# Tree attention on one core: four V copies two steps later, and 768 KB of the last stores moved from SyncE's queue to GpSimd's

## The chip, the cores and the metric

The kernel runs on one core of one Trainium2 chip. A core has TensorE (PE in the profile; its weight loads are PEld), VectorE (DVE), ScalarE (ACT), GpSimd (POOL) and SyncE (SP), which run their own queues of instructions and meet through semaphores, and 16 DMA engines that move data between device memory and the core's memories. GpSimd, SyncE and ScalarE issue the transfers; those of GpSimd go through one software queue, those of SyncE and ScalarE through a hardware queue each. The metric is the device time of one execution in microseconds. Before the change it is 134.9 us, the median of 3 runs (134.57 to 135.15).

## What is computed

Attention over 8 x 12 = 96 heads of 512 positions and 64 dimensions, where position i may attend only to itself and to its ancestors in a binary tree (the parent of i is (i - 1) // 2):

```python
scores = np.einsum('bhqd,bhkd->bhqk', Q, K) * scale
scores = scores + (1 - mask) * (-1e9)          # mask[i, j] = 1 for j = i and i's ancestors
weights = np.exp(scores - np.max(scores, axis=-1, keepdims=True))
weights = weights / (np.sum(weights, axis=-1, keepdims=True) + 1e-10)
return np.einsum('bhqk,bhkd->bhqd', weights, V).astype(np.float32)
```

Q, K, V and the output are float32, 12.6 MB each.

## The kernel before, in words

**Pairs and steps.** The 96 heads are taken as 48 pairs. From pair 8 on the heads of two neighbouring pairs are interleaved, so that pairs 2n and 2n + 1 fill the four heads 4n to 4n + 3, and pair 2n has the first and third of them. One step of the main loop (variable `i`, 0 to 48) does, on PE, the scores of pair i (`scores1`, `scores2`: codes for the mask, L458 and L491, and keys times queries, L466 and L501), then the value products of pair i - 1 (`values`, L551), then the turn (transposition) of K or Q for two pairs: in an odd step i the K of pairs i + 3 and i + 4 (`wide_k`, L401), in an even step the Q of pairs i + 2 and i + 3 (`wide_q`, L433). ScalarE takes the exponentials (L476, L507). VectorE normalizes pair i - 1 (`norm`: reciprocal L581, product L582), copies the turned K or Q out of PSUM (L412, L416, L420 for K, L441 for Q), and does its share of the V copies. There is one PSUM buffer for the value products, so the products of pair i wait for the normalization of pair i - 1.

**V copies.** The schedule is written out by hand; each engine takes its instructions in the order in which the program issues them. V is loaded in blocks of 16 heads (8 pairs), in three pieces by partition ("upper", "even", "odd"), and then rearranged by `spread` (L336) into value tiles that PE reads; block o serves pairs 8o to 8o + 7. There are two sets of value tiles, used in turn. `BY_VECTOR` and `BY_SCALAR` say which copies are issued in which step for blocks 0 to 3; from block 4 on `STEADY_VECTOR` and `STEADY_SCALAR` do, by the step's number modulo 8, for the block after the one whose step it is. "M" (reads all three pieces) and "Y" (reads "even" and "odd") are VectorE's, "Z0" and half of "Z1" (both read "upper") ScalarE's. GpSimd makes the "top" copies, "X", which overwrites part of what M wrote and so comes after both halves of M, and half of "Z1".

**GpSimd's queue.** `pool_program` is the list of all loads, GpSimd's V copies and most stores, in one fixed order; `ready` says from which step on the head of that list may be issued. Loads cast float32 to bfloat16 on the way. K and Q are loaded 8 heads at a time (`load_k`, `load_q`, L251), V by `load_rows` (L280). Eight semaphores serve this queue in turn, so that each transfer is issued only when the one issued eight before it has landed.

**Stores.** `norm` writes a quad of four heads (two pairs), 512 KB, kept in one of 22 buffers. `store` (L590) writes a quad, or some of its heads, to device memory. GpSimd stores quads 0 to 21 but for quad 19, at first between loads and 56 heads behind, the rest one after another at the end of its list. Quad 19 (pairs 38 and 39) is stored by SP at step 41 in two transfers by rows, 60 and 68 of the 128 (`store_apart`, L600 to L606). The pairs 44, 45 and 46 are each stored by SP as soon as they are normalized (256 KB each, steps 45 to 47), and the two heads of pair 47 by SP and by ScalarE.

Of the kernel before, what the change touches and what calls it, by code (L numbers as in the profile page):

```python
# [119 lines left out]
def kernel(  # L120
# [7 lines left out]
    nc = tc.nc  # L128
    B, H, S, D = Q.shape
    P = nc.NUM_PARTITIONS  # L130
    assert S == 512 and D == 64 and P == 128 and (B * H) % 4 == 0
    scale = float(1.0 / np.sqrt(D))
    NH = B * H
    NQ = NH // 4
    NP = 2 * NQ
    WIDE = 8
    KB, VB = 8, 16
# [14 lines left out]
    Or = out.rearrange("b h (p t) d -> p (b h) (t d)", t=4)  # L152
# [58 lines left out]
    NV = 2  # L211
# [17 lines left out]
    qTs, kTs, kqs, obs, ets, ofs = {}, {}, {}, {}, {}, {}  # L229
# [224 lines left out]
    def scores1(i):  # L454

        sp = psS.tile([P, 2, 512], fp32, name="s1")
        for a in range(2):
            nc.tensor.matmul(  # L458
                out=sp[:, a, :],
                lhsT=(k1code if i < WIDE else k1wide)[64 * a:64 * a + CODE_ROWS, :],  # L460
                rhs=(q1code[64 * a:64 * a + CODE_ROWS, :] if i < WIDE
                     else q1wide[64 * a:64 * a + CODE_ROWS, :, :]),
                start=True, stop=False,
            )
        for a in range(2):
            nc.tensor.matmul(  # L466
                out=sp[:, a, :], lhsT=keys(i, a, TOP),
                rhs=qTs[i][64 * a:64 * a + 64, :, :].rearrange("p t c -> p (t c)"),
                start=False, stop=True,
            )  # L470
        et = etpool.tile([P, 2, 4, 128], bf16, name="e1")
        nc.scalar.activation(  # L472
            out=et[:, :, :, :].rearrange("p a t c -> p (a t c)"),
            in_=sp[:, :, :].rearrange("p a c -> p (a c)"),
            func=AF.Exp, scale=scale,
        ) if i < WIDE else nc.scalar.activation(  # L476
            out=et[:, :, :, :].rearrange("p a t (r u) -> p a (t r) u", u=2),
            in_=sp[:, :, :].rearrange("p a (u c) -> p a c u", u=2),
            func=AF.Exp, scale=scale,
        )  # L480
        ets[i] = et
# [31 lines left out]
    def scores2(i):  # L513
        if i >= WIDE:
            return scores2_wide(i)
        sp = psS.tile([P, 2, 4, 128], fp32, name="s2")
        flat = sp[:, :, :, :].rearrange("p a t c -> p a (t c)")
        for a in range(2):
            nc.tensor.matmul(
                out=sp[:, a, :, 32:128], lhsT=k2code[64 * a:64 * a + CODE_ROWS, :],  # L520
                rhs=q2code[64 * a:64 * a + CODE_ROWS, :].rearrange(
                    "p (t c) -> p t c", t=4
                )[:, :, 32:128],
                start=True, stop=False,
            )
        for t, lo, hi in ((2, 32, 192), (0, 192, 256), (3, 288, 448), (1, 448, 512)):
            for a in range(2):
                nc.tensor.matmul(
                    out=flat[:, a, lo:hi], lhsT=keys(i, a, TILE2[t]),
                    rhs=qTs[i][64 * a:64 * a + 64, :, :].rearrange("p t c -> p (t c)")[:, lo:hi],  # L530
                    start=False, stop=t == 1, skip_group_check=t in (2, 3),
                )
        nc.scalar.activation(
            out=e2s[i % NE][:, :, :, 32:128].rearrange("p a t c -> p (a t) c"),
            in_=sp[:, :, :, 32:128].rearrange("p a t c -> p (a t) c"),
            func=AF.Exp, scale=scale,
        )
# [59 lines left out]

    APART, APART_AT, APART_ROWS = 19, 41, 60

    def store_apart():  # L600

        for p0, p1 in ((0, APART_ROWS), (APART_ROWS, P)):
            nc.sync.dma_start(
                out=Or[p0:p1, 4 * APART:4 * APART + 4, :],
                in_=ofs[APART][p0:p1, :, :, :].rearrange("p h t d -> p h (t d)"),
            )  # L606

    def pool_program():

        ops = [  # L610
            (load_k, 2, 2), (load_q, 2, 2), (load_v, 0, 4), (load_v, 4, 4),
            (load_k, 4, 2), (load_k, 6, 2), (load_q, 4, 2), (load_k, 8, 4),
            (load_q, 6, 2), (load_q, 8, 4), (load_v, 8, 8), (load_k, 12, 4),
            (load_q, 12, 4), (load_k, 16, 4), (load_rows, 1, "upper"),
            (load_q, 16, 4), (load_rows, 1, "even"), (load_k, 20, 4), (load_rows, 1, "odd"),
            (load_q, 20, 4), (load_k, 24, 8), (load_q, 24, 4), (load_rows, 2, "upper"),
            (load_q, 28, 4), (load_k, 32, 4), (load_rows, 2, "even", "odd"),
            (load_q, 32, 8), (load_k, 36, 4), (load_rows, 3, "upper"),
            (load_k, 40, 8), (load_q, 40, 8),
            (load_rows, 3, "even", "odd"), (spread_top, 2, 0, 16), (spread_top, 3, 0, 4), (load_q, 48, 4),  # L620
            (spread_top, 3, 4, 8), (load_k, 48, 8), (load_q, 52, 4), (spread_top, 3, 8, 12),
            (load_rows, 4, "upper"), (spread_top, 3, 12, 16),
        ]
        loaded, stored = 72, 0
        for h in range(56, NH, KB):
            top = [(spread_top, h // VB + 0)] if h % VB == 8 and 4 <= h // VB + 0 < NH // VB else []
            ops += [(load_k, h, KB)] + top + [(load_q, h, KB)]
            while loaded < min(h + 32, NH):
                names = ("even", "odd") if loaded % VB else ("upper",)
                ops.append((load_rows, loaded // VB) + names)  # L630
                loaded += KB
            if top:
                o = h // VB
                ops.append((spread_pool, (o, "X", 0, 16), (o, "Z1", 8, 16)))
            while 4 * stored + 4 + BEHIND <= h + KB:
                ops.append((store, nc.gpsimd, stored))
                stored += 1
        ops += [(store, nc.gpsimd, q) for q in range(stored, NQ - 2) if q != APART]
        return ops

    def ready(op, i):

        f, args = op[0], op[1:]
        if f in (load_k, load_q):
            return 2 * (i + 3) >= args[0] + args[1] - 4 * KB
        if f is load_v:
            return True
        if f is load_rows:
            return 2 * i >= VB * (args[0] - 2)
        if f is spread_pool:  # L650
            return 2 * i >= VB * (args[0][0] + 1 - NV) + 6
        if f is spread_top:
            return 2 * i >= VB * (args[0] + 1 - NV)
        return 2 * i >= 4 * (args[1] + 1)
# [21 lines left out]
        22: [(3, "Y", 0, 8)],  # L676
        23: [(3, "X", 8, 16)],
        24: [(3, "Y", 8, 16)],
    }
    BY_SCALAR = {  # L680
# [18 lines left out]
    }  # L699

    STEADY_VECTOR = {0: [("M", 0, 8)], 2: [("M", 8, 16)], 4: [("Y", 0, 8)], 6: [("Y", 8, 16)]}
# [2 lines left out]
    def spread_by(copy, table, steady, i):  # L704

        o, j = divmod(i, 8)
        todo = table.get(i, [])
        if 4 <= o + 1 < NH // VB:
            todo = todo + [(o + 1,) + piece for piece in steady.get(j, [])]
        for args in todo:  # L710
            spread(copy, *args)
# [25 lines left out]
    for i in range(NP + 1):  # L737
        steps = FIRST[i] if i < len(FIRST) else "SVK" if i % 2 else "SVQ"
        for step in steps:
            if step == "S" and i < NP:  # L740
                scores1(i)
                scores2(i)
            if step == "V" and i >= 1:
                values(i - 1)
                norm(i - 1)
                valued = True
            if step == "K" and kdone < NP:
                kdone = turn("kst", kdone)
            if step == "Q" and qdone < NP:
                qdone = turn("qst", qdone)  # L750
            if step == "W":
                nc.scalar.copy(
                    out=codes[64:64 + CODE_ROWS, 1280:1536], in_=codes[0:CODE_ROWS, 1280:1536]
                )
            if step == "X":
                spin("s1" if valued else "ob", 2)
            if step == "D":
                spread_by(nc.vector.tensor_copy, BY_VECTOR, STEADY_VECTOR, i)
            if step == "A":
                spread_by(nc.scalar.copy, BY_SCALAR, STEADY_SCALAR, i)  # L760
        if "D" not in steps:
            spread_by(nc.vector.tensor_copy, BY_VECTOR, STEADY_VECTOR, i)
        if "A" not in steps:
            spread_by(nc.scalar.copy, BY_SCALAR, STEADY_SCALAR, i)
        pool(i)
        if i == APART_AT:
            store_apart()
        if i >= NP - 3 and i < NP:
            store(nc.sync, (i - 1) // 2, (i - 1) % 2, 2, 2)
    assert not program  # L770
    store(nc.sync, NQ - 1, 1, 1)
# [31 lines left out]
```

## Time and profile before

| what | value |
|---|---|
| median of 3 runs | 134.9 us (134.57 to 135.15) |
| the profiled execution's own time | 134.59 us |
| its span, first to last instruction | 132.7 us |
| busy: PE / VectorE / ScalarE / GpSimd | 115.9 / 101.8 / 102.3 / 70.8 us |
| device memory read and written | 37.94 and 12.58 MB, 381 GB/s over the span |
| granted clock of TensorE, mean | 0.962 |
| last matmul ends | 127.15 us from the span's start |
| last store is issued (ScalarE) | 128.42 us |

The profile is of one execution. Its times count from the first instruction. A row of a timeline has the start, the time taken, the engine, the line of the kernel, the operation, what it writes and reads, how many were merged, and in brackets how long the engine stood idle ahead of it and what ended that. "PEclk" is the clock granted to TensorE, in tenths of full speed in the slices and as a fraction in the windows. "DMA share" is the busy time of the 16 DMA engines over the stretch; it can be above 1 where packets overlap. GB/s counts the bytes as written, so that a load from float32 to bfloat16 counts half of what is read.

### The profile page before, as it was taken

The page shows a single profiled execution, that of the slowest core. Times are in us where ns is not written, and L with a number is a line of the kernel's source. Part 1 is how long each engine was busy: PE and PEld are TensorE (multiplying, and loading weights), DVE is VectorE, ACT ScalarE, POOL GpSimd, SP SyncE. Part 2 cuts the span into 40 slices and gives each one's busy share as a digit, 9 for nine tenths or more (in the row PEclk, how much of TensorE's full clock was granted, in tenths as well). Part 3 has the DMA queues.
Part 4 walks back from the last instruction along what each step waited for, and adds up shares of the span by engine and source line. Part 5 has one row for each costly group of instructions (what it writes and reads, how often), then busy time and mean ns, then how long its engine had stood idle before and what let it go on. Part 6 is the DMA issues. An engine that isn't in the chain of part 4 may idle for free.

```text
span 132.7 us, 5554 instructions
## 1 busy us (share of the span) xinstructions
PE 115.9 (87%) x2414; PEld 80.5 (61%) x2417; DVE 101.8 (77%) x253; ACT 102.3 (77%) x169; POOL 70.8 (53%) x110
## 2 busy tenths in 40 slices
PE   6986979999899999999989399999999997979930
PEld 2453755766675666677767267767767675656620
DVE  3439779889999999988985655888987977756360
ACT  4359577988799999979899536997997987695910
POOL 6989625355345808999413359863958524422000
PEclk9999999999999999999999756999999999999995
DMA  3999999999999999999999999999999999999992
GB/s 113 237 179 194 200 196 200 201 202 206 200 202 202 203 202 206 199 207 201 207 202 198 307 264 201 281 285 240 327 218 328 239 292 399 405 394 406 360 332 87
DMA packets 32381, 32.27 MB, mean 243 GB/s; under 512 B 1341, under 2 KB 29629, under 8 KB 32357
## 3 DMA queue, kind: packets, MB, share of 16 engines
q0 software_dynamic: 29984, 29.63, 114.4%
q1 hardware_dynamic: 1813, 1.83, 4.0%
q10 hardware_dynamic: 560, 0.46, 1.1%
q8 instruction: 19, 0.31, 0.9%
q14 instruction: 5, 0.04, 0.1%
HBM read 37.94 MB, written 12.58 MB: 381 GB/s over the span
## 4 chain that ended last, share of the span: by engine, by line
DMA 42%; PE 39%; issue 6%; ACT 4%; POOL 3%; DVE 2%; ACTq 0%; POOLq 0%
DMA vst<-in_V_dram 35%; PE ob L551 12%; DMA kst<-in_K_dram 7%; PE s L458 6%; PE ktp L401 4%; PE s L466 4%; PE qtp L433 3%; PE s L491 3%; PE s L501 3%; ACT e L507 2%; ACT e L476 2%; DVE of L582 1%; PE s L551 1%; ACT e L472 1%; DVE vt L336 1%
## 5 line engine op out<-in xcount | busy, mean ns | idle before, releaser
L476 ACT ACTIVATE e<-s 128x1024 bf16<-128x1024 f32 x40 | 40.8, 1019 | 15.1 <-PE s L466 14.8
L551 PE MATMUL ob<-vt,e 128*128 128x65 bf16 (+1 forms) x940 | 38.2, 199 | 4.8 <-DVE of L582 2.9
L551 PEld LDWEIGHTS <-e 128*128 128x128 bf16 (+1 forms) x960 | 31.0, 104 | 13.0 <-DVE of L582 3.1
L507 ACT ACTIVATE e<-s 128x384 bf16<-128x384 f32 x80 | 34.4, 486 | 0.0
L582 DVE TENSOR_TENSOR of<-ob,rec 128x512 f32<-128x512 f32 x47 | 32.5, 691 | 1.6
L590 POOL DMA_DIRECT2D out_dram<-of x21 | 16.0, 763 | 16.1 <-DVE of L582 5.0
L336 DVE COPY vt<-vst 32x1024 bf16<-32x1024 bf16 (+6 forms) x46 | 19.5, 425 | 5.5 <-issue 2.8
L458 PE MATMUL s<-codes 40*128 40x512 bf16 x96 | 19.9, 401 | 1.2 <-ACT e L472 0.4
L581 DVE RECIPROCAL rec<-ob 128x8 f32<-128x8 f32 x47 | 9.7, 206 | 13.7 <-PE ob L551 13.2
L336 POOL COPY vt<-vst 32x128 int32<-32x128 int32 (+2 forms) x32 | 15.7, 490 | 6.9 <-DMA vst<-in_V_dram 4.0
L466 PE MATMUL s<-kq 64*128 64x512 bf16 x96 | 19.0, 385 | 0.0
L280 POOL DMA_DIRECT2D vst<-in_V_dram x15 | 11.1, 742 | 10.5 <-DMA vst<-in_V_dram 6.1
L336 ACT COPY vt<-vst 32x512 int32<-32x512 int32 (+3 forms) x29 | 15.9, 550 | 1.0 <-DMA vst<-in_V_dram 0.5
L501 PEld LDWEIGHTS <-kq 64*128 64x128 bf16 x320 | 12.7, 95 | 4.5 <-issue 0.7
L501 PE MATMUL s<-kq 64*128 64x160 bf16 (+1 forms) x320 | 15.2, 210 | 0.0
L491 PE MATMUL s<-codes 40*128 40x384 bf16 x80 | 14.1, 339 | 0.9
L251 POOL DMA_DIRECT2D kst<-in_K_dram x12 | 9.0, 753 | 10.4 <-PE s L466 3.4
L401 PE MATMUL ktp<-ptile,kst 128*64 128x128 bf16 x320 | 12.9, 224 | 1.2 <-issue 0.8
L441 DVE COPY kq<-qtp 128x1024 bf16<-128x1024 bf16 x20 | 13.6, 681 | 0.0
L491 PEld LDWEIGHTS <-codes 40*128 40x128 bf16 x80 | 6.6, 96 | 11.0 <-issue 3.8
L433 PE MATMUL qtp<-ptile,qst 128*64 128x128 bf16 x320 | 13.1, 224 | 0.2 <-issue 0.2
L251 POOL DMA_DIRECT2D qst<-in_Q_dram x13 | 9.5, 731 | 5.7 <-PE s L501 3.0
(42 smaller groups left out, 123.8 us busy)
## 6 DMA issues: line engine op xcount, KB each, us to landing
out_dram<-of POOLq DMA_DIRECT2D x21, 512.0 KB, 12.6
kst<-in_K_dram POOLq DMA_DIRECT2D x8, 512.0 KB, 13.3
qst<-in_Q_dram POOLq DMA_DIRECT2D x7, 512.0 KB, 13.8
vst<-in_V_dram POOLq DMA_DIRECT2D x12, 256.0 KB, 13.0
vst<-in_V_dram POOLq DMA_DIRECT2D x6, 512.0 KB, 12.7
qst<-in_Q_dram POOLq DMA_DIRECT2D x8, 256.0 KB, 10.8
kst<-in_K_dram POOLq DMA_DIRECT2D x6, 256.0 KB, 11.6
out_dram<-of SPq DMA_DIRECT2D x3, 256.0 KB, 5.0
```

The costliest lines, as they stand in the source:

```text
L251: return nc.gpsimd.dma_start(out=kept[b][:, h0 % KB:h0 % KB + n, :, :].rearrange("p (g x) t d -> p g (x t d)", x=2), in_=wide[:, h0 // 2:( ...
L336: return copy(out=dst, in_=src)
L401: nc.tensor.transpose(out=columns(kp[64 * a:64 * a + 64, :], mixed, (256, 2), (leaves - mixed, 2), (1, 32)), in_=st[:, 2 * i % KB // 2 + a ...
L433: nc.tensor.transpose(out=halves[64 * a:64 * a + 64, :, c:c + 64], in_=st[:, 2 * i % KB // 2 + a, 4 * u + t, :], identity=ptile[:, 0:128],)
L458: nc.tensor.matmul(out=sp[:, a, :], lhsT=(k1code if i < WIDE else k1wide)[64 * a:64 * a + CODE_ROWS, :], rhs=(q1code[64 * a:64 * a + CODE_ ...
L466: nc.tensor.matmul(out=sp[:, a, :], lhsT=keys(i, a, TOP), rhs=qTs[i][64 * a:64 * a + 64, :, :].rearrange("p t c -> p (t c)"), start=False, ...
L476: ) if i < WIDE else nc.scalar.activation(
L491: nc.tensor.matmul(out=flat[:, a, :, :].rearrange("p u (t c) -> p u t c", t=4)[:, :, :, 16:64], lhsT=k2wide[64 * a:64 * a + CODE_ROWS, :], ...
L501: nc.tensor.matmul(out=flat[:, a, :, lo:hi], lhsT=keys(i, a, WTILE2[t]), rhs=qT[64 * a:64 * a + 64, :, lo:hi], start=False, stop=t == 1, s ...
L507: nc.scalar.activation(out=e2s[i % NE][:, a, :, 32:128].rearrange("p t (r u) -> p t r u", u=2), in_=flat[:, a, :, :].rearrange("p u (t r) ...
L551: nc.tensor.matmul(out=ob[lo:hi, a, 65 * t:65 * t + 65], lhsT=e[:, a, PLACE[t], lo:hi], rhs=vt[vtile[tile_v][0]][:, head(i, a) % VB, vtile ...
L582: nc.vector.tensor_tensor(out=ofs[q][:, head(i, a) % 4:head(i, a + n - 1) % 4 + 1:head(i, 1) - head(i, 0), :, :], in0=o4[:, a:a + n, :, 0: ...
```

## The change

Two things change, and nothing is computed differently.

First, VectorE's four copies of block 4 (heads 64 to 79, pairs 32 to 39). They were issued in steps 24, 26 (the halves of M), 28 and 30 (the halves of Y) by the steady table; now they are in `BY_VECTOR` at steps 26, 28, 30 and 31. ScalarE's three copies of block 4 are written out in `BY_SCALAR` at their old steps 25, 27 and 29. The steady tables begin with block 5. GpSimd's X and Z1 pieces of blocks 4 and 5 are issued one step later (`+ 8` in place of `+ 6`).

Second, the stores. Quad 22 (pairs 44 and 45) is stored by GpSimd, as the last of its list, in one transfer of 512 KB instead of two of 256 KB by SP. Of quad 19 SP stores only the first two heads, in the same 60 and 68 rows; GpSimd stores the other two heads at quad 19's place in its list, in three transfers of 9, 116 and 3 rows. SP keeps pair 46 and one head of pair 47.

```diff
+    def store_rows(eng, q, h0, *bounds):
+
+        for p0, p1 in zip(bounds, bounds[1:]):
+            eng.dma_start(
+                out=Or[p0:p1, 4 * q + h0:4 * q + h0 + 2, :],
+                in_=ofs[q][p0:p1, h0:h0 + 2, :, :].rearrange("p h t d -> p h (t d)"),
+            )
+
     def store_apart():
 
-        for p0, p1 in ((0, APART_ROWS), (APART_ROWS, P)):
-            nc.sync.dma_start(
-                out=Or[p0:p1, 4 * APART:4 * APART + 4, :],
-                in_=ofs[APART][p0:p1, :, :, :].rearrange("p h t d -> p h (t d)"),
-            )
+        store_rows(nc.sync, APART, 0, 0, APART_ROWS, P)
...
-        ops += [(store, nc.gpsimd, q) for q in range(stored, NQ - 2) if q != APART]
+        for q in range(stored, NQ - 1):
+            if q == APART:
+                ops.append((store_rows, nc.gpsimd, q, 2, 0, 9, 125, P))
+            else:
+                ops.append((store, nc.gpsimd, q))
         return ops
...
         if f is spread_pool:
-            return 2 * i >= VB * (args[0][0] + 1 - NV) + 6
+            return 2 * i >= VB * (args[0][0] + 1 - NV) + 8
...
         24: [(3, "Y", 8, 16)],
+        26: [(4, "M", 0, 8)],
+        28: [(4, "M", 8, 16)],
+        30: [(4, "Y", 0, 8)],
+        31: [(4, "Y", 8, 16)],
     }
     BY_SCALAR = {
...
+        25: [(4, "Z0", 0, 8)],
+        27: [(4, "Z0", 8, 16)],
+        29: [(4, "Z1", 0, 8)],
     }
...
-        if 4 <= o + 1 < NH // VB:
+        if 5 <= o + 1 < NH // VB:
             todo = todo + [(o + 1,) + piece for piece in steady.get(j, [])]
...
-        if i >= NP - 3 and i < NP:
+        if i == NP - 1:
             store(nc.sync, (i - 1) // 2, (i - 1) % 2, 2, 2)
```

## The prediction

> **What bounds the kernel now.** I read the page's slices first, because they show at once whether one resource is full throughout. Each figure is one fortieth of the span, 3.3 us.
>
> ```profile
> PEclk9999999999999999999999756999999999999995
> DMA  3999999999999999999999999999999999999992
> GB/s 113 237 179 194 200 196 200 201 202 206 200 202 202 203 202 206 199 207 201 207 202 198 307 264 201 281 285 240 327 218 328 239 292 399 405 394 406 360 332 87
> HBM read 37.94 MB, written 12.58 MB: 381 GB/s over the span
> ```
>
> The DMA engines are full from the second slice to the last but one. Loads show some 200 GB/s because 4 bytes are read for 2 written; stores alone show 400. So the transfers bound the kernel, and a stall of PE costs time only if it still shows at the end. The slices also show one dip of the granted clock. The timelines of VectorE, PE and GpSimd around it:
>
> ```profile
> 74.13 0.43 DVE L336 COPY vt<-vst 128x1024 bf16<-128x1024 bf16 x1 [2.43 <-issue]
> 75.46 1.20 PE L551 MATMUL ob<-vt,e 128*128 128x65 bf16 x20 [2.32 <-DVE of L582]
> 78.51 0.75 POOL L251 DMA_DIRECT2D kst<-in_K_dram  x1 [0.81 <-PE s L466]
> ```
>
> VectorE waited 2.43 us at the V copy ("M", block 4) of step 24. The page calls the cause "issue", but the piece of V that it reads, issued at 60.7, landed 13.3 us later, at 74.0. Behind it in VectorE's queue stood the normalization, and PE's next value products waited 2.32 us for that. The third line is a load of K that comes back below. Then the windows, cut where the clock changes:
>
> ```profile
> 6.71:13.53 6.82, 5.18 (x87) 3.00 (x86) 4.67 (x12) 5.37 (x8) 6.04 (x9) 1.00 1.41 187
> 68.15:74.97 6.82, 4.99 (x113) 3.58 (x109) 3.91 (x11) 6.08 (x11) 2.69 (x4) 1.00 1.39 215
> 74.97:81.80 6.83, 6.34 (x90) 4.50 (x92) 4.68 (x12) 2.26 (x4) 4.03 (x7) 0.50 1.19 268
> ```
>
> Columns: length, busy time of PE, weight loads, VectorE, ScalarE and GpSimd, then clock, DMA share, GB/s. After the window with PE busy 4.99 us the clock was 0.50 for 6.83 us; after 5.18 us it stayed at 1.00. The chain from 75.5 to the end is PE, then the last normalization and store. Last, the tail, in windows of 1 us, and the queues that feed it:
>
> ```profile
> 125.00:126.00 1.00, 1.00 (x30) 0.76 (x24) 0.12 (x1) 1.00 (x2) 0.00 (x0) 1.00 0.84 307
> 127.00:128.00 1.00, 0.15 (x4) 0.04 (x4) 0.80 (x5) 0.00 (x0) 0.00 (x0) 1.00 0.83 308
> 129.00:130.00 1.00, 0.00 (x0) 0.00 (x0) 0.00 (x0) 0.00 (x0) 0.00 (x0) 0.79 0.82 279
> 130.00:131.00 1.00, 0.00 (x0) 0.00 (x0) 0.00 (x0) 0.00 (x0) 0.00 (x0) 0.50 0.37 127
> 121.21 0.75 POOL L590 DMA_DIRECT2D out_dram<-of  x1 [4.33 <-DVE of L582]
> 125.15 3.06 SPq L590 DMA_DIRECT2D out_dram<-of  x3
> ```
>
> Here alone the DMA engines have gaps: stores come too late or lie unevenly.
>
> **V copies later.** Nothing is added: four VectorE copies of block 4 move from steps 24, 26, 28, 30 to 26, 28, 30, 31. ScalarE's three keep their steps. Without the wait PE runs on from 73.14 (75.46 less 2.32). Value products and the Q turn take 1.17 us at full clock (82.33 to 83.50), so step 27 starts at 74.3 instead of 77.45; a step is 2.1 us (90.16, 92.25, 94.36), so step 29 starts at 78.5 instead of 83.50. PE would be 5.0 us ahead. The moved M copy comes after the normalization and Q copy of step 26, about 75.5, and its data is there at 74.0.
>
> What is late next is the loads, which don't move: GpSimd issues each as an earlier landing frees one of eight places, so the full DMA queue sets their times. Issue plus time to landing, against the turn on PE that needs it, before: K of pairs 32 to 35 at 81.6, used 85.07, slack 3.4; Q of these 84.2 against 87.17, 2.9; K of pairs 36 to 39 at 91.9 (78.51 + 13.4) against 93.82, 1.9; Q of these 94.6 (81.80 + 12.8) against 95.91, 1.3; K of 40 to 43, 3.0; Q, 2.6; of 44 to 47, 4.2 and 4.7. So PE waits some 1.5 us at step 29, 0.5 at 30, 1.1 to 1.5 at 33, 0.5 at 34, and from there is 1.3 us ahead, not 5. **Term: -1.3 us** for PE's end, between 0 (the lead is lost) and 1.3.
>
> Step 31 has now a V copy beside the three K copies: 0.24 + 0.61 + 3 x 0.33 + 0.42, 2.3 us against 2.1; the 0.2 us vanish in PE's wait of step 33. GpSimd's X copy of block 4 waits for M of step 28, at about 79.7; GpSimd reached it at 82.59, so nothing. Block 5's two GpSimd pieces are placed a step later in the program, but GpSimd's own order is the same: nothing. There X waited for VectorE (1.42 us idle ahead of 98.12); PE's lead takes that away, and the store issue behind it finds a full queue: nothing.
>
> **Stores.** SP loses pairs 44 and 45 (two of 256 KB) and half of the four heads of pairs 38 and 39; GpSimd gets 768 KB in four issues more, 4 x 0.75 = 3.0 us. GpSimd is free there (idle 4.33 us before 121.21, nothing after 122), so they cost its time only. But each takes one of eight places: pairs 40, 41 now wait for the landing that came at 120.8 and go at 121.1 instead of 116.14, 42, 43 at 122.4, 44, 45 at 123.8 (normalized at 125.1 less 1.3); nothing stands behind that last one on GpSimd. The queue then still holds work: the store issued at 114.67 landed 11.3 us later, at 126.0. That covers the delay; without that cover the 5 us would show. SP's half store waits for the normalization of pair 39 as before, and the store of pair 46 behind it is not due for 15 us.
>
> Price of moved bytes: the SP queue's 4.0% of 16 engines x 132.7 us for 1.83 MB is 46 ns per KB; the stretch 110 to 117, mostly GpSimd stores, 1.04 x 16 x 7 us for 2.81 MB, 41 ns. 768 KB x 5 ns / 16 = 0.2 us gained. If 2 KB runs cost like SP's, 0.16; both too small to show by themselves. How the 9, 116 and 3 rows lie on the 16 engines no row shows; from both sides: at best they fill the tail's gaps, at worst engines that get more finish later (rival below). I take nothing for it, between.
>
> From 125.0 on 1,724 KB are left in the windows; at the 398 GB/s of 117 to 124 that is 4.3 us, so transfers could end at 129.3. PE's term puts the last store at 127.1 (128.42 - 1.3), and it landed 3.1 us after its issue: 130.2. PE's end decides, by 0.9 us.
>
> **Sum.** Profiled execution 134.59 (span 132.7, 1.9 around it) - 1.3 = 133.3. The median of the runs is 134.9, 0.3 above that execution: **133.6 us**. Own range 133.0 (transfers packed to 129.5) to 134.2.
>
> [...]
>
> **Rivals.** (1) Slower: PE's new waits close the clock once more. In 88.6 to 95.5 PE would idle 1.6 to 2.0 us, busy 4.8 to 5.2, just between the row that closed (4.99) and the one that did not (5.18). It decides below about 5.1. Half clock for 6.83 us costs 3.4 us; PE is then 2.1 behind instead of 1.3 ahead, past all loads' slack: 134.9 + 2.1 = 137.0. Against it: the waits come in pieces, while the closing gap was one of 2.32 us. [...]
> (2) No change: it closes earlier, after the wait of step 29 (74.97 to 81.80, busy about 5.3), which eats the lead where PE would have waited anyway; or the last engines drain as before. 134.6.
> (3) Slower by the tail: the 116 rows lie on few engines. On four of the sixteen each had 29 rows of 2 KB, 58 KB, and 58 x 41 ns = 2.4 us more to do; less 0.7 for SP's smaller half, and then three stores at the 1.7 us between the landings of the last two (127.3, 129.0): 126.0 + 1.7 + 5.1 = 132.8 instead of 131.5, 136.2 us. It decides once that landing is past 131.5.
>
> **Numbers.** Forecast 0.54, (2) 0.18, (1) 0.19, (3) 0.09. Less than 0.5% (0.7 us) can't be told from no change here. Faster 0.54, same 0.18, slower 0.28. The range reaches from 133.0 to 136.3 and leaves out (1).
>
> **What would show it.** Right: no V copy waits over 1 us near 72; clock 1.00 from 75 to 82; PE waits for kst and qst at about 80 and 91; last matmul near 125.9; windows from 125 to 129 at share 1. Wrong: a clock dip after 82 or 95.5; GpSimd's last store landing after SP's; PE's end early and the last landing not.

## The result, and the profile after

The changed kernel takes 136.53 us (median of 5 runs, 135.99 to 136.74) against 134.87 us; the ratio is 1.0103, 95% interval 1.0066 to 1.0139. It is slower by 1%, where 133.6 us and a gain were forecast, and outside the stated range by 0.2 us. Medians here are over all executions while the ratios leave disturbed ones out, so the two can differ, most for the run with 12 and 116 rows below. Of each time some part lies outside the span from the first to the last instruction: 1.7 to 2.1 us in most executions of these kernels and 2.8 to 3.5 in the others, the kernel before among them. The spans, which are on record for every execution, therefore tell small differences better: the five of the change have 134.0 to 134.9 us (median 134.7), and those of the kernel before have a median of 132.8 us in each session of the experiments below.

The slices of the page after (span 134.8 us, one slice is 3.4 us):

```profile
PEclk9999599999999999999999999999999999999975
DMA  2999999999999999999999999999999999999950
GB/s 97 244 178 195 196 200 199 203 205 202 201 199 206 200 203 205 200 205 199 206 202 203 341 224 201 330 236 296 275 249 320 222 364 400 399 405 344 382 202 35
```

The dip of the clock in the middle is gone. (There is one early in this execution, in the fifth slice, where the clock was 0.50 from 13.8 to 17.2 us. It made PE late: the turn of step 23 began at 73.70, and before at 71.60.) But the last two slices show 202 and 35 GB/s, where before they were 332 and 87. Two timelines, of VectorE and PE, answer to those of the wait before:

```profile
77.97 0.42 DVE L336 COPY vt<-vst 128x1024 bf16<-128x1024 bf16 x1
82.19 0.42 DVE L336 COPY vt<-vst 128x1024 bf16<-128x1024 bf16 x1
...
93.11 0.64 PE L401 MATMUL ktp<-ptile,kst 128*64 128x128 bf16 x16
95.62 0.58 PE L433 MATMUL qtp<-ptile,qst 128*64 128x128 bf16 x14 [0.19 <-DMA qst<-in_Q_dram]
124.84 1.25 PE L551 MATMUL s<-vt,e 128*128 128x65 bf16 x20
```

Neither M copy waits any more. PE now just meets the loads: the K of pairs 36 to 39 landed at 93.0 (78.74 + 14.3) and its turn starts at 93.11; the Q landed at 95.5 (82.04 + 13.5) and its turn waits until 95.62. PE ends at 126.09, 1.1 us earlier than the 127.15 before, although it was 2.1 us late at step 23. So the first half of the change did what it says. The windows (length, busy time of PE, weight loads, VectorE, ScalarE, GpSimd, then clock, DMA share, GB/s) show where the time went instead:

```profile
68.15:74.97 6.82, 6.49 (x146) 4.70 (x148) 6.32 (x15) 6.33 (x12) 2.54 (x4) 1.00 1.39 210
74.97:81.80 6.83, 6.49 (x152) 4.61 (x147) 5.72 (x15) 5.72 (x12) 3.97 (x7) 1.00 1.19 272
...
128.00:129.00 1.00, 0.00 (x0) 0.00 (x0) 0.00 (x0) 0.00 (x0) 0.00 (x0) 1.00 1.01 364
129.00:130.00 1.00, 0.00 (x0) 0.00 (x0) 0.00 (x0) 0.00 (x0) 0.00 (x0) 0.93 0.56 203
130.00:131.00 1.00, 0.00 (x0) 0.00 (x0) 0.00 (x0) 0.00 (x0) 0.00 (x0) 0.50 0.27 103
131.00:132.00 1.00, 0.00 (x0) 0.00 (x0) 0.00 (x0) 0.00 (x0) 0.00 (x0) 0.50 0.25 92
132.00:133.00 1.00, 0.00 (x0) 0.00 (x0) 0.00 (x0) 0.00 (x0) 0.00 (x0) 0.50 0.19 67
```

From 130 to 133 the DMA share is 0.27, 0.25 and 0.19: the work of four, four and three of 16 engines, with nothing left for the others. The packet records of the trace say the same twice more. From 130 to 131 us exactly four packets are in flight during 0.68 us, from 131 to 132 during 0.80, and never fewer than four in either. And besides the 128 packets of 4 KB of each of its 22 whole stores, GpSimd's queue has 56 packets of 4 KB and 16 of 2 KB. That is what 29 rows on each of four engines give, 14 times two rows and one left over, with the 9 and 3 rows single; the run below with one transfer of 128 rows has 64 of 4 KB and none of 2 KB. This is GpSimd's issuing, with the store of pairs 36, 37 first and then the three transfers of pairs 38, 39 (L603):

```profile
115.34 0.75 POOL L590 DMA_DIRECT2D out_dram<-of  x1 [0.62 <-DVE of L582]
116.98 0.60 POOL L603 DMA_DIRECT2D out_dram<-of  x1 [0.88 <-DVE rec L581]
118.47 1.89 POOL L603 DMA_DIRECT2D out_dram<-of  x2 [0.90 <-DMA out_dram<-of]
...
124.36 0.75 POOL L590 DMA_DIRECT2D out_dram<-of  x1 [1.03 <-DVE of L582]
```

The store ahead landed 10.6 us after its issue, at 125.9; the 116 rows, issued at 118.47, landed 9.8 us later, at 128.3. That is 2.4 us for 232 KB, which at 400 GB/s take 0.6. The last store of the list landed at 132.8 (124.36 + 8.4), SP's two last at 133.3 (125.91 + 7.4) and 133.5 (126.80 + 6.7), where the last landing before was at 131.5. Between the two profiles the span grew by 2.1 us, from 132.7 to 134.8.

### The profile page after: what moved, and what is told of

The parts are those of the page before. It is cut to its first block, busy times and chain, and to the rows that moved or that the text cites. A ratio compares the mean times of both kernels' runs of the same rounds, so it can differ in the third digit from the quotient of the medians.

```text
span 134.8 us, 5556 instructions
## 1 busy us (share of the span) xinstructions
PE 115.4 (86%) x2414; PEld 79.8 (59%) x2417; DVE 102.1 (76%) x253; ACT 102.5 (76%) x169; POOL 73.9 (55%) x114
## 4 chain that ended last, share of the span: by engine, by line
PE 45%; DVE 20%; DMA 15%; ACT 6%; issue 4%; POOL 4%; ACTq 0%; POOLq 0%
PE ob L551 16%; DMA qst<-in_Q_dram 10%; DVE of L582 7%; PE s L458 7%; DMA vst<-in_V_dram 5%; DVE vt L336 5%; PE ktp L401 4%; PE s L466 4%; PE qtp L433 4%; PE s L501 3%; PE s L491 3%; DVE rec L581 2%; DVE kq L441 2%; POOL vt L336 2%; ACT e L507 2%
## 5 line engine op out<-in xcount | busy, mean ns | idle before, releaser
L590 POOL DMA_DIRECT2D out_dram<-of x22 | 16.9, 769 | 14.1 <-DMA qst<-in_Q_dram 3.7
L336 DVE COPY vt<-vst 32x1024 bf16<-32x1024 bf16 (+6 forms) x46 | 20.0, 436 | 2.4 <-DMA vst<-in_V_dram 1.7
## 6 DMA issues: line engine op xcount, KB each, us to landing
kst<-in_K_dram POOLq DMA_DIRECT2D x8, 512.0 KB, 13.8
qst<-in_Q_dram POOLq DMA_DIRECT2D x7, 512.0 KB, 14.3
qst<-in_Q_dram POOLq DMA_DIRECT2D x8, 256.0 KB, 10.6
kst<-in_K_dram POOLq DMA_DIRECT2D x3, 128.0 KB, 6.8
```

What stands on the lines that cost most here:

```text
L336: return copy(out=dst, in_=src)
```

## The experiments

**The two halves, each alone.** First the V copies: the change with the stores of before.

```diff
-        store_rows(nc.sync, APART, 0, 0, APART_ROWS, P)
+        for p0, p1 in ((0, APART_ROWS), (APART_ROWS, P)):
+            nc.sync.dma_start(... all four heads, as before)
...
-        for q in range(stored, NQ - 1):
...
+        ops += [(store, nc.gpsimd, q) for q in range(stored, NQ - 2) if q != APART]
...
-        if i == NP - 1:
+        if i >= NP - 3 and i < NP:
             store(nc.sync, (i - 1) // 2, (i - 1) % 2, 2, 2)
```

> The V copies of the change alone, the stores as before. Theory (the three transfers of 9, 116 and 3 rows lay two heads on a few DMA engines, which then end late): the V copies are the good part; the last matmul ends about 1.1 us earlier than before and the time is 133.8 to 134.6 us. Rival (PE's lead itself hurts, because it moves stores or loads against each other): 135.5 us or more.

Measured: 134.91 us, ratio to before 1.0015 (0.9975 to 1.0055): no difference. Neither expectation holds. In its profile the clock is 1.00 from the start to 125.9. Two turns of PE's, its last products and the last store are

```profile
82.03 0.64 PE L401 MATMUL ktp<-ptile,kst 128*64 128x128 bf16 x16 [0.43 <-DMA kst<-in_K_dram]
92.92 0.64 PE L401 MATMUL ktp<-ptile,kst 128*64 128x128 bf16 x16 [1.68 <-DMA kst<-in_K_dram]
123.80 1.25 PE L551 MATMUL s<-vt,e 128*128 128x65 bf16 x20
126.31 0.35 ACTq L590 DMA_DIRECT2D out_dram<-of  x1
```

so PE waits for the loads of K at the turns of steps 29 and 33, ends at 125.05, 2.1 us earlier than before, and the last store is issued at 126.31 instead of 128.42. It then takes 5.5 us to land, at 131.8, where it took 3.1 before and landed at 131.5. The whole lead turned into waiting in the DMA queues. (Not all of the 2.1 us is the copies': with the copies at their old steps PE ended at 125.96 and 126.28 in two runs below, where the clock was half for 3.4 us and not for 6.8.)

Then the stores alone: the kernel before with the four edits on stores.

```diff
         if f is spread_pool:
-            return 2 * i >= VB * (args[0][0] + 1 - NV) + 8
+            return 2 * i >= VB * (args[0][0] + 1 - NV) + 6
...
-        26: [(4, "M", 0, 8)],
...
-        if 5 <= o + 1 < NH // VB:
+        if 4 <= o + 1 < NH // VB:
```

> The stores of the change alone, the V copies as before, so that VectorE waits and the clock halves. Theory: few engines end late whatever PE does; 136.3 to 137.3 us, with windows at a DMA share of 0.2 to 0.6 in the last 3 to 4 us before the last landing. Rival (PE's lead hurts): about 134.9 us.

Measured: 136.75 us, ratio 1.0129 (1.0072 to 1.0185). Its spans have a median of 134.7 us, as those of the change. All of the loss is in the stores, and it is there whether VectorE waits or not.

**The same stores in even rows.** GpSimd's two heads of pairs 38 and 39 in one transfer of 128 rows:

```diff
-                ops.append((store_rows, nc.gpsimd, q, 2, 0, 9, 125, P))
+                ops.append((store_rows, nc.gpsimd, q, 2, 0, P))
```

> The change, but GpSimd's two heads of pairs 38 and 39 go in one transfer of 128 rows instead of 9, 116 and 3. Theory: the weight on few engines is gone, GpSimd's last store lands by about 130.5, and the time is 133.4 to 134.3 us. Rival 1 (it is the number of issues and the places they take): also near 134. Rival 2 (pairs 44 and 45 come too late in GpSimd's queue): 136 us or more.

Measured: 134.92 us, ratio 1.0004 (0.9965 to 1.0043). The loss is gone; the gain that the theory then left for PE's lead is not there. Its last windows:

```profile
128.00:129.00 1.00, 0.00 (x0) 0.00 (x0) 0.00 (x0) 0.00 (x0) 0.00 (x0) 0.50 0.78 288
129.00:130.00 1.00, 0.00 (x0) 0.00 (x0) 0.00 (x0) 0.00 (x0) 0.00 (x0) 0.50 0.60 214
130.00:131.00 1.00, 0.00 (x0) 0.00 (x0) 0.00 (x0) 0.00 (x0) 0.00 (x0) 0.50 0.15 51
131.00:132.00 1.00, 0.00 (x0) 0.00 (x0) 0.00 (x0) 0.00 (x0) 0.00 (x0) 0.50 0.01 2
```

The three microseconds at a quarter share are gone. But the engines still end at different times between 128 and 131, although the last store was issued at 126.30.

With three transfers in row counts that sixteen divides, as many issues as in the change:

```diff
-                ops.append((store_rows, nc.gpsimd, q, 2, 0, 9, 125, P))
+                ops.append((store_rows, nc.gpsimd, q, 2, 0, 48, 80, P))
```

> The change, but with three transfers of 48, 32 and 48 rows instead of 9, 116 and 3: as many issues and places, in row counts that sixteen divides. Theory (weight): within 0.4 us of the run with one transfer of 128 rows. Rival 1 (issues and places): as the change, 136.0 to 136.7 us.

Measured: 134.85 us, ratio 0.9996 (0.9962 to 1.0029). Its 48, 32 and 48 rows would be 3, 2 and 3 on each of 16 engines, and the trace has the 32 packets of 2 KB that this gives. So neither the two more issues nor the places that they take cost anything that can be told; the row counts do.

**The weight twice.** All four heads of pairs 38 and 39 by GpSimd, in 9, 116 and 3 rows for each two heads, and none by SP:

```diff
                 ops.append((store_rows, nc.gpsimd, q, 2, 0, 9, 125, P))
+                ops.append((store_rows, nc.gpsimd, q, 0, 0, 9, 125, P))
...
-        if i == APART_AT:
-            store_apart()
```

> The change, but all four heads of pairs 38 and 39 go by GpSimd in 9, 116 and 3 rows, two heads after the other, and SP stores none of them: the suspected weight twice. If both 116 rows fall on the same four engines (9 + 4 + 3 make sixteen, so the count starts over), these carry 116 KB, 4.8 us at 41 ns per KB, less the SP rows that they lose where they had any: 138 to 139.5 us, with a share near 0.25 for some 5 us. If the weight is not the cause, about the change's 136.5 us.

Measured: 139.40 us, ratio 1.0346 (1.0307 to 1.0385). The tail of its profile:

```profile
131.00:132.00 1.00, 0.00 (x0) 0.00 (x0) 0.00 (x0) 0.00 (x0) 0.00 (x0) 0.50 0.75 295
132.00:133.00 1.00, 0.00 (x0) 0.00 (x0) 0.00 (x0) 0.00 (x0) 0.00 (x0) 0.50 0.26 99
133.00:134.00 1.00, 0.00 (x0) 0.00 (x0) 0.00 (x0) 0.00 (x0) 0.00 (x0) 0.50 0.26 100
134.00:135.00 1.00, 0.00 (x0) 0.00 (x0) 0.00 (x0) 0.00 (x0) 0.00 (x0) 0.50 0.15 57
```

Twice the weight costs 2.9 us more than once, and again some four engines end alone. In all it is 4.6 us above the kernel before, near the 4.8 us that 116 KB take at 41 ns per KB. Why the first 116 rows cost less than the second is not shown; that the first filled what slack there was is one way.

**Where the weight lies.** If the four engines are taken in turn, the order and size of the small transfers choose which four. Three variants, one line each:

```diff
-                ops.append((store_rows, nc.gpsimd, q, 2, 0, 9, 125, P))
+                ops.append((store_rows, nc.gpsimd, q, 2, 0, 116, 125, P))    # 116, 9, 3 rows
+                ops.append((store_rows, nc.gpsimd, q, 2, 0, 4, 120, P))      # 4, 116, 8 rows
+                ops.append((store_rows, nc.gpsimd, q, 2, 0, 12, P))          # 12, 116 rows
```

> The change with the three transfers in the order 116, 9, 3 rows: the same counts on the same number of engines, but if few engines are taken in turn, on others than in the order 9, 116, 3. Theory A (a weight of 232 KB on four engines is too much wherever it lies): 136 to 137 us. Theory B (it is too much only on the engines that the order 9, 116, 3 picks): below 135.5 us. In both the windows of the last 2 to 3 us show a share near 0.25 if it is late at all.

> The change with 4, 116 and 8 rows instead of 9, 116 and 3: if four engines are taken in turn, the 116 rows fall on the four behind those of the order 116, 9, 3. The landing of the 116 rows after that of the store ahead of them tells how far those four are behind: 2.4 us (all of 58 KB at 41 ns per KB) if one of them is the slowest, as with 9, 116, 3 (2.36 us); about 0.6 us if they are ahead, as with 116 first (0.56 us). Time 136 to 137 us in the first case, 135 to 135.6 us in the second.

> The change with two transfers of 12 and 116 rows instead of 9, 116 and 3: by the same count the 116 rows fall on the last four engines. Landing of the 116 rows 2.4 us after the store ahead and 136 to 137 us if one of these is the slowest; about 0.6 us and 135 to 135.6 us if they are ahead.

In the table the second column is the landing of the 116 rows less that of the 512 KB store ahead of them, each as issue plus time to landing, in the one profiled execution.

| rows, in order | 116 rows after the store ahead | median | ratio to before | spans (of the profiled one) |
|---|---|---|---|---|
| 116, 9, 3 | 126.8 - 126.2 = 0.6 us | 135.51 us | 1.0038 (1.0003 to 1.0073) | 133.1 to 134.3 (133.1) |
| 12, 116 | 127.2 - 126.2 = 1.0 us | 136.62 us | 1.0083 (1.0036 to 1.0129) | 133.4 to 133.9, 134.7 to 135.1, 136.3 (133.7) |
| 4, 116, 8 | 128.0 - 126.2 = 1.8 us | 136.69 us | 1.0128 (1.0060 to 1.0197) | 133.7 to 134.9 (134.8) |
| 9, 116, 3 (the change) | 128.3 - 125.9 = 2.4 us | 136.53 us | 1.0103 (1.0066 to 1.0139) | 134.0 to 134.9 (134.8) |

The place matters: with 116 first every span but one is below the shortest of the change. 58 KB an engine at 41 ns per KB are 2.4 us. With 9, 116, 3 all of it shows, in the stores alone and in the first two heads of the double weight too (2.4 us each), so among those four is one that had no time to spare; with 116 first only 0.6 us show, so in that execution those four were at least 1.8 us ahead of the slowest. The expectations for the other two knew only all or little; 1.0 and 1.8 us lie between. Those two can't be told apart: the executions with 12, 116 fall into groups, and the profile is of one in the fastest. That it is a place counted on by each transfer, and that 12, 9, 4 and 3 rows take as many engines, is supposed and not seen: no record of these profiles names the engine. The table, in which the place depends on the transfers ahead, fits it but does not prove it.

**What sets the end.** With 512 KB less to store, that is, the change with pairs 38 and 39 not stored at all and their four heads left out of the output:

```diff
-            if q == APART:
-                ops.append((store_rows, nc.gpsimd, q, 2, 0, 9, 125, P))
-            else:
+            if q != APART:
                 ops.append((store, nc.gpsimd, q))
...
-        if i == APART_AT:
-            store_apart()
```

> The change, with the four heads of pairs 38 and 39 not stored at all (their 512 KB of output are left out). Theory (with the V copies later and even stores the DMA engines set the end and PE's lead is worth nothing): 512 KB at 400 GB/s is 1.3 us, so 133.3 to 133.8 us against the 134.9 of the run with one transfer of 128 rows. Rival (the end is PE's, the last store's issue and its landing): no lower than that run, 134.6 to 135.0 us.

Measured: 133.31 us, ratio 0.9870 (0.9822 to 0.9917), 1.4 us below before and 1.6 below the kernel with one transfer of 128 rows. 512 KB at 400 GB/s are 1.3 us. By itself this does not rule the rival out, for PE ended earlier too (124.11, against 125.05 with one transfer of 128 rows) and the last store landed 4.9 us after its issue in both. The next run moves PE and not the bytes.

The stores with 128 rows, but the V copies at their old steps:

```diff
-        26: [(4, "M", 0, 8)],
...
-        if 5 <= o + 1 < NH // VB:
+        if 4 <= o + 1 < NH // VB:
...
-                ops.append((store_rows, nc.gpsimd, q, 2, 0, 9, 125, P))
+                ops.append((store_rows, nc.gpsimd, q, 2, 0, P))
```

> The change's stores with one transfer of 128 rows, but the V copies at their old steps, so that VectorE waits and the clock halves. Theory (the DMA engines set the end): within 0.5 us of the run with the V copies later, 134.5 to 135.4 us. Rival (PE's lead is worth its 1.3 us as predicted and something else took as much): 135.8 us or more.

Measured: 134.81 us, ratio 1.0012 (0.9976 to 1.0048), the same as with the V copies later. Its profile still has the wait and the half clock:

```profile
73.94 0.43 DVE L336 COPY vt<-vst 128x1024 bf16<-128x1024 bf16 x1 [2.53 <-issue]
76.22:79.63 3.41, 3.41 (x52) 2.25 (x49) 1.87 (x5) 1.92 (x4) 2.04 (x3) 0.50 1.16 269
127.55 0.35 ACTq L590 DMA_DIRECT2D out_dram<-of  x1
```

(a row of VectorE's timeline, a window, a row of ScalarE's). The last store is issued at 127.55, 1.25 us later than with the V copies late, and lands 4.1 us after that, at 131.7; with the V copies late it landed 4.9 us after 126.30, at 131.2. In the profiles of all seven kernels that store everything and have no transfer of 116 rows, the last store was issued between 126.30 and 128.75 and the last landing came between 131.5 and 131.8. With the run that stores less, this says that the transfers set the end.

**SP's 60 and 68 rows, and pairs 44 and 45.** SP's two heads in one transfer of 128 rows too:

```diff
-        store_rows(nc.sync, APART, 0, 0, APART_ROWS, P)
+        store_rows(nc.sync, APART, 0, 0, P)
```

> The change with both halves of pairs 38 and 39 in one transfer of 128 rows each, SP's too, so that no transfer of the tail lies on fewer than all engines. If the 60 and 68 rows of SP put weight on engines that had time to spare, this is slower than the run with SP's two pieces, 135.2 us or more; if they were too much, it is faster, 134.2 to 134.7 us.

Measured: 135.46 us, ratio 1.0025 (0.9993 to 1.0057). By the ratios this can't be told from SP's 60 and 68 rows (1.0004), as the intervals overlap. The spans say slower: a median of 133.6 us over 12 executions, where that run had 133.0 and the kernel before 132.8. So SP's uneven rows lay, if anything, where there was time to spare. Its profile is of its fastest execution (span 132.5). There the clock closed early, PE ended at 127.48, later than in any other run, and the last store was issued at 128.75 and landed 2.8 us later. And pairs 44 and 45 by GpSimd with the V copies later, while pairs 38 and 39 stay with SP as before:

```diff
-            if q == APART:
-                ops.append((store_rows, nc.gpsimd, q, 2, 0, 9, 125, P))
-            else:
+            if q != APART:
                 ops.append((store, nc.gpsimd, q))
```

> The change without its part on pairs 38 and 39: V copies later, pairs 44 and 45 by GpSimd, and all four heads of pairs 38 and 39 by SP in 60 and 68 rows as before. Theory (only the 9, 116 and 3 rows cost): no slower than the runs with even rows, 134.4 to 135.0 us; at best the 0.2 us that the cheaper GpSimd bytes promise. Rival (pairs 44 and 45 as one late store cost part of the time): 135.4 us or more.

Measured: 134.88 us, ratio 1.0008 (0.9970 to 1.0046). Storing pairs 44 and 45 from GpSimd costs nothing and gains nothing. No version tried that computes all of the output beats the kernel before by more than can be told.

## Why the prediction was wrong

**V copies later: the mechanism right, its worth wrong.** The wait of 2.43 us and the half clock went. With the V copies alone PE waited 0.43, 0.24, 1.68 and 0.21 us for the loads at the turns of steps 29, 30, 33 and 34, where 1.5, 0.5, 1.1 to 1.5 and 0.5 were worked out; the change's own profile, late from its early half clock, shows only 0.19 us at step 34. PE ended 1.1 us earlier in the change and 2.1 us with the V copies alone, for 1.3 forecast; against the two other runs with the copies at their old steps, the V copies alone gained 0.9 and 1.2 us. The step that failed is the one behind it: "PE's end decides, by 0.9 us". The end was put where PE's last store would land, 3.1 us after its issue, because that is what the store took before. That 3.1 us was not a property of the store. Issued earlier, it took 4.1 to 5.5 us, for the engines were still busy, and issued later 2.8.

**The transfers' own end was put 2 us too early.** That "transfers could end at 129.3" shared the bytes left after 125 among all 16 engines at the full rate. No run that stores everything came near: with the row counts even and every store issued by 126.3 the last packets ran until 131, since the engines do not end together (shares of 0.78, 0.60 and 0.15 from 128 to 131 with one transfer of 128 rows). The gaps that I read in the tail before as "stores come too late or lie unevenly" were mostly the second, as far as these runs tell. The mean share over 16 engines hides which of them is last, and the last one sets the end.

**The 9, 116 and 3 rows: left at nothing.** "I take nothing for it, between" is the term that failed. It measured 1.3% with the stores alone and 1.0% in the whole change. Rival (3) had the mechanism and the price right: 2.4 us for 58 KB on each of four engines (measured 2.4 between the landings). That its last landing of GpSimd's, 132.8 us, was also measured as 132.8 is luck in part: it took 0.7 us off for SP's smaller half, which did not show, and gave the three stores behind 5.1 us, where they took 4.5 (from 128.3 to 132.8). Its 136.2 us stands against 136.53. It was given 0.09. That four engines would carry the 116 rows was supposed: no row of the kernel before shows it, and the change's trace does (shares of 0.27 and 0.25). Nor did any row show whether those four had slack; the run with the order 116, 9, 3 shows that some had (0.6 us between the landings, for 2.4).

**What held.** The four more issues on GpSimd and the places that they take are free (48, 32 and 48 rows: 0.9996). Rival (1) did not come. In the change's profile PE was late and busy 6.71 us in the window from 88.63 to 95.46; but with the V copies alone it was busy 5.11 us from 88.39 to 95.21, and with the weight twice 4.82 from 88.74 to 95.57, below the 5.1 at which the rival was to decide, and the clock stayed at 1.00 in both. Rival (2), no change, is what the V copies alone do, and for the second of its two reasons, that the last engines drain as before; the first, a closing of the clock after step 29, did not come.

## What to carry to other kernels

Here the DMA engines were full almost to the end (in the kernel before a share of 90% or more in every slice up to 129.4 us but the first, in a span of 132.7), and a stall of a compute engine was worth nothing, however well its removal worked (ratio 1.0015 with the V copies alone). Whether a stall is worth anything can be asked directly, by leaving out a known number of bytes and by moving the compute alone; it takes both, for leaving out bytes can move the compute too (here PE's end, from 125.05 to 124.11). A DMA share below 1 in the last microseconds can be read as a number of engines: here 0.25 was four packets in flight, four of sixteen engines at work, behind a transfer of 116 rows, where 128 rows in one transfer (ratio 1.0004) or 48, 32 and 48 in three (0.9996) cost nothing that can be told. The time that the last store takes from issue to landing is no constant to add to an earlier issue, as long as there is a queue ahead of it: it was 2.8 to 5.5 us here.

## What the runs showed of the hardware

As far as the landings tell, engines are not equally far behind: with the order 116, 9, 3 the 116 rows, 2.4 us of work on each of four, landed 0.6 us after the store ahead in the profiled execution, and with 9, 116, 3 all 2.4 us after it, in three profiles.

How long PE was busy does not by itself say whether the clock closes. Counted over 6.8 us, it closed after PE had been busy 4.99 us (before) and 4.57 us (early in the change's execution), but stayed open after 4.66 us (4, 116, 8 rows) and 4.82 us (the weight twice), and near the end of the V copies alone it closed after 5.65 us, 0.9 us behind PE's last product. These are the window of the change, those of the last three runs in this order, and the last 3.41 us ahead of the closing before:

```profile
6.98:13.81 6.83, 4.57 (x68) 2.53 (x66) 4.21 (x11) 4.96 (x8) 5.67 (x8) 1.00 1.42 187
4.91:11.74 6.83, 4.66 (x74) 2.79 (x76) 4.04 (x10) 5.00 (x8) 6.58 (x10) 1.00 1.40 188
88.74:95.57 6.83, 4.82 (x116) 3.44 (x110) 4.70 (x12) 4.64 (x10) 3.91 (x7) 1.00 1.17 276
119.11:125.94 6.83, 5.65 (x113) 3.82 (x108) 3.78 (x11) 5.19 (x9) 0.75 (x1) 1.00 1.02 396
71.56:74.97 3.41, 1.58 (x38) 1.01 (x36) 0.95 (x4) 3.11 (x7) 1.94 (x3) 1.00 1.41 231
```

So the forecast's bound of about 5.1 us, between the 4.99 that closed and the 5.18 that did not, was no bound; what else decides, these runs do not show.

The early closing is in two of the fourteen profiles (the change's and that with SP's 128 rows) and did not set the end in the second, for the transfers ran on meanwhile. In the kernel before the clock closed at 74.97, 1.83 us into the wait that began at 73.14, after 3.41 us in which PE was busy for 1.58.
